# Graph attention on one core: the closing scaling and store, one destination block at a time

## The chip, the cores and the metric

The kernel runs on one core of a Trainium2 chip. Its engines work side by side, each on its own queue of instructions: TensorE (PE in the profile, with its weight loads as PEld), VectorE (DVE), ScalarE (ACT), GpSimd (POOL) and SyncE (SP), which here only issues DMAs. The metric is the device time of one execution in microseconds (us).

## The reference

A graph has 4096 nodes with 64 features and 50,000 edges. For each of 4 heads the features are projected (64 to 64), every edge gets a score from its two ends, and each destination node receives the average of its sources' projections, weighted with the exponential of the score:

```python
for h in range(n_heads):
    x_proj[h] = x @ weight[h]
    src_att = np.sum(x_proj[h, src_nodes] * att_src[h], axis=-1)
    dst_att = np.sum(x_proj[h, dst_nodes] * att_dst[h], axis=-1)
    edge_scores[h] = src_att + dst_att
edge_scores = np.where(edge_scores > 0, edge_scores, 0.2 * edge_scores)
...
        output[h, dst] += np.exp(edge_scores[h, i]) * x_proj[h, src]
...
            total = np.sum(np.exp(edge_scores[h, edges_to_dst]))
            output[h, dst] /= (total + 1e-8)
return output.transpose(1, 0, 2).reshape(num_nodes, -1)
```

So the result is a matrix of 4096 rows (destinations) by 256 columns (4 heads of 64), in 32-bit floats.

## The kernel before

The first half of the time goes into sorting the edges by destination, on VectorE. The second half, where the change lies, walks over the destinations in 33 blocks (`ND`) of 125 (`BD`); block 32, the last, has 96. Since the weighted average commutes with the projection, the kernel sums the weighted features first (`acc`) and projects the sum of each block afterwards.

`Blocks.run` is the loop over the blocks; one turn `b` of it is called step `b` here. The order is written out by hand: each engine takes its instructions in the order in which the code names them, and the steps of different blocks are interleaved.

- `load(b + 4)` has SyncE issue a DMA of 1 MB into a tile `bc` (four buffers): the sorted edges of a later block, spread over all partitions.
- `onehot(b + 2)` lets VectorE turn `bc` into matrices of zeros and ones (`oh`), in two parts: L471 for the first 4096 columns, L474 for the other 2048.
- `gather(b + 1, c)`, in three chunks `c`, lets TensorE multiply these with the node tables (L492, L494, L498) into `ps`. ScalarE takes the exponentials from it (`ex`, L500) and copies the features (`xs`, L502).
- `weights(b + 1)` picks the edge weight (`wv`, L512) and `values(b)` multiplies it with the features (`val`, L520), both on VectorE.
- `sums(b, -1)` adds up the weights on TensorE (L538); `sums(b, 0)` and `sums(b, 1)` add up the weighted features into `acc`, 32 products in all (L545). ScalarE then copies `acc` into `aT` (L602, `take`). In block 32 these go through other tiles, in parts.

What is done with a finished block is in the class `Finish`. `project(b - 1)`, placed in step `b` behind the first chunk of the gather, has TensorE multiply `aT` with the weights into the tile `pf` (L606). `invert` takes the reciprocals of the summed weights on VectorE (`inv`, L611), `give` multiplies `pf` with them into `res` on VectorE (L618) and issues the stores of the result (L622): on SyncE's queue, and for the last block one half on SyncE's and one on ScalarE's.

Before the change a tile `aT`, `pf`, `inv` or `res` holds two blocks. `project` runs in each step and fills one half of `pf`; `invert` and `give` run in the even steps from step 2 on, for blocks `b - 2` and `b - 1` together. `pf` has a single buffer (the pool `ps_f`, `bufs=1`), while `aT`, `inv` and `res` have two (the pool `fin`, `bufs=2`). When a buffer is taken anew, its writer waits for the last reader of what it held.

Inside a step, VectorE's order is: `val`, reciprocal (even steps), first part of `oh`, `wv`, second part of `oh`, scaling (even steps). Steps 1 to 3 add four small instructions at their end, which unpack the windows of later blocks (L416 to L420). TensorE's order is: first chunk of the gather, projection, sums of the weights, second and third chunk, sums of the features.

The functions that the diff touches are used once more, in a part that runs only if the edges are spread so unevenly that a window overflows; with these inputs it is not entered. The class `Total` belongs to that part.

Of the kernel before, what the change touches and what calls it, by code (L numbers as in the profile page):

```python
# [11 lines left out]
P = 128  # L12
ALPHA = 0.2
F32 = mybir.dt.float32
BF16 = mybir.dt.bfloat16
I32 = mybir.dt.int32
OP = mybir.AluOpType
# [10 lines left out]
BD = 125  # L28
# [4 lines left out]
def av(a, off, *dims):  # L33

    return dataclasses.replace(a, offset=a.offset + off, ap=[list(a.ap[0])] + [list(d) for d in dims])
# [3 lines left out]
def kernel(ctx: ExitStack, tc: tile.TileContext, x: bass.AP, edge_index: bass.AP,  # L39
                         weight: bass.AP, att_src: bass.AP, att_dst: bass.AP, out: bass.AP):  # L40
    nc = tc.nc
    V, S, G, T = nc.vector, nc.scalar, nc.gpsimd, nc.tensor
    N, Din = x.shape
    H, _, Dout = weight.shape
    E = edge_index.shape[1]
    NB = N // P
    ND = -(-N // BD)
    NI = -(-ND // 8)
    SG = N // NR
    C = H * Dout  # L50
# [122 lines left out]
    Wbd = cst.tile([P, 2, P], F32)  # L173
# [7 lines left out]
    class Sorter:  # L181


        def __init__(self, pool, first):
            self.a = [first, pool.tile([P, L], F32, name="sA"), pool.tile([P, L], F32, name="sB")]
            self.cur = 0
            self.y = pool.tile([P, L], F32, name="sY")
            self.z = pool.tile([P, L], F32, name="sZ")
# [121 lines left out]
    def whole(pool, t, up, what):  # L310

        i = pool.tile([P, NI], I32, name=f"whole{what}")
        V.tensor_scalar(out=i[:], in0=t[:], scalar1=float(up), scalar2=None, op0=OP.add)
        V.tensor_scalar(out=i[:], in0=i[:], scalar1=FINE, scalar2=FINE, op0=OP.logical_shift_right,
                        op1=OP.logical_shift_left)
        V.tensor_copy(out=t[:], in_=i[:])
# [26 lines left out]
    def group(pool, pp, start, spy=None):  # L343

        raw = pool.tile([P, L], F32, name="raw")
        fetch(pool, skey1, start, W1, raw, 1)
        kr = pool.tile([P, L], F32, name="kr")
        S.activation(out=kr[:], in_=raw[:], func=ACTF.Identity, bias=goff[:, 0:1])
        sgn = below(pool, kr[:], L, nb2, ND, 8 * NI)
        so = Sorter(pool, raw)  # L350
        so.rows(9)
        cps = counts(pool, pp, sgn, 8 * NI, [sel2[:]])
        ki = pool.tile([P, L], I32, name="ki")
        store(skey2, so.runs(ki, FINE, spy))
        bounds(pool, cps, 8 * NI, L, off2, m8, 8, ws2, we2)
        whole(pool, ws2, 0, 0)
# [46 lines left out]
    AW = 2 * BD + H  # L403
# [26 lines left out]
    class Blocks:  # L430
# [129 lines left out]
        def run(self, first=0, also={}):  # L560
            for b in range(first, ND):
                self.load(b + 4)
                self.values(b, 2 if b == ND - 1 else 1)
                self.gather(b + 1, 0)
                if b:
                    self.sink.project(b - 1)
                self.sums(b, -1)
                self.gather(b + 1, 1)
                self.gather(b + 1, 2)

                pair = b and b % 2 == 0
                if pair:
                    self.sink.invert(b - 2, 2)
                self.onehot(b + 2, halves=(0,))
                self.weights(b + 1)
                self.onehot(b + 2, halves=(1,))
                if pair:
                    self.sink.give(b - 2, 2)
                self.sums(b, 0)
                self.sums(b, 1)  # L580
                if b in also:
                    also[b]()
            self.sink.project(ND - 1)
            n = 2 - ND % 2
            self.sink.invert(ND - n, n)
            self.sink.give(ND - n, n, 2)

    class Finish:


        def __init__(self, ctx):
            self.first = eps
            self.apart = True
            self.aT, self.pf = {}, {}
            self.fp = ctx.enter_context(tc.tile_pool(name="fin", bufs=2))
            self.psf = ctx.enter_context(tc.tile_pool(name="ps_f", bufs=1, space=PSUM))

        def take(self, b, acc, at=0):
            if b % 2 == 0 and acc.shape[-1] != BD:
                self.aT[b // 2] = self.fp.tile([P, 2, AW], F32, name="aT")  # L600
                self.pf[b // 2] = self.psf.tile([P, 2, C], F32, name="pf")
            S.copy(out=self.aT[b // 2][:, b % 2, at:at + acc.shape[-1]], in_=acc)  # L602

        def project(self, b):
            for k in range(2):
                T.matmul(out=self.pf[b // 2][:, b % 2, k * P:(k + 1) * P], lhsT=self.aT[b // 2][:, b % 2, k * BD:k * BD + P],  # L606
                         rhs=Wbd[:, k, :], start=(b % 2 == 0 and k == 0), stop=True, skip_group_check=True)

        def invert(self, b, n):
            self.inv = self.fp.tile([P, 2, H], F32, name="inv")  # L610
            V.reciprocal(out=self.inv[0:BD, 0:n], in_=self.aT[b // 2][0:BD, 0:n, 2 * BD:AW])  # L611

        def give(self, b, n, parts=1):
            res = self.fp.tile([P, 2, H, Dout], F32, name="res")
            nh = H // parts
            for k, eng in zip(range(parts), (nc.sync, nc.scalar)):
                h = slice(k * nh, (k + 1) * nh)
                V.tensor_tensor(out=res[0:BD, 0:n, h], in0=av(self.pf[b // 2][0:BD], k * nh * Dout, [C, n], [Dout, nh], [1, Dout]),  # L618
                                in1=av(self.inv[0:BD], k * nh, [H, n], [1, nh], [0, Dout]), op=OP.mult)
                for i in range(n):  # L620
                    m = min(BD, N - (b + i) * BD)
                    eng.dma_start(out=out[(b + i) * BD:(b + i) * BD + m, k * nh * Dout:(k + 1) * nh * Dout],  # L622
                                  in_=res[0:m, i, h].rearrange("p h o -> p (h o)"))

    class Total:

# [9 lines left out]
        def project(self, b):  # L636
            pass

        def invert(self, b, n):
            pass  # L640

        def give(self, b, n, parts=1):
            pass

    def advance(pool, ws, we, w, what):

        n = ws.shape[1]
        at = pool.tile([P, n], F32, name=f"at{what}")
        gone = pool.tile([P, n], F32, name=f"gone{what}")
        V.tensor_tensor(out=gone[:], in0=ws[:], in1=we[:], op=OP.is_ge)  # L650
        V.tensor_scalar(out=at[:], in0=ws[:], scalar1=-1.0, scalar2=float(P * L), op0=OP.mult, op1=OP.add)
        V.tensor_tensor(out=at[:], in0=at[:], in1=gone[:], op=OP.mult)
        V.tensor_tensor(out=at[:], in0=at[:], in1=ws[:], op=OP.add)
        V.tensor_scalar(out=ws[:], in0=ws[:], scalar1=float(w), scalar2=None, op0=OP.add)
        return at
# [86 lines left out]
    with tc.If((n1 > W1) | (n2 > W2)):  # L742
        with tc.tile_pool(name="all", bufs=1) as al:
            total = al.tile([P, ND, AW], F32)
            V.memset(total[:], 0.0)
            with tc.For_i(0, n1, W1):
                at1 = advance(al, ws1, we1, W1, 1)
                with tc.tile_pool(name="sort3", bufs=1) as so3, tc.tile_pool(name="pp3", bufs=1, space=PSUM) as pp3:
                    group(so3, pp3, at1[:])
                    whole(so3, we2, (1 << FINE) - 1, 1)  # L750
                    longest(so3, pp3, (ws2, we2))
                m2 = room(1, L)
                with tc.For_i(0, m2, W2):
                    with ExitStack() as st:
                        win = Windows(st.enter_context(tc.tile_pool(name="win", bufs=1)), advance(al, ws2, we2, W2, 2)[:])
                        for i in range(NI):
                            win.unpack(i, nc.sync, nc.scalar)
                        blocks = Blocks(st, Total(total))
                        for b in range(4):
                            blocks.load(b)  # L760
                        blocks.onehot(0)
                        blocks.start()
                        blocks.run()
            with ExitStack() as st:
                V.tensor_scalar(out=total[:, :, 2 * BD:AW], in0=total[:, :, 2 * BD:AW], scalar1=1e-8, scalar2=None,
                                op0=OP.add)
                fin = Finish(st)
                for b in range(ND):
                    fin.take(b, total[:, b, :])
                    fin.project(b)  # L770
                    if b % 2 or b == ND - 1:
                        fin.invert(b - b % 2, b % 2 + 1)
                        fin.give(b - b % 2, b % 2 + 1)


# [28 lines left out]
```

## Time and profile before

| | us |
|---|---|
| median of 14 runs | 298.91 |
| lowest and highest of them | 295.94 and 300.15 |
| the profiled execution's own time | 296.66 |
| its span, from the first to the last instruction | 294.7 |

| engine | busy us | share of the span |
|---|---|---|
| PE (products) | 202.6 | 69% |
| PEld (weight loads) | 193.7 | 66% |
| VectorE | 260.6 | 88% |
| ScalarE | 186.0 | 63% |
| GpSimd | 28.1 | 10% |

The profile shows one execution. It divides the span into 40 equal slices and prints the busy share of each engine in tenths, 9 for 90% or more; PEclk is the clock granted to TensorE in the same tenths. A group of instructions is one line of the code on one engine: what it writes and reads, how often it ran, its busy time and the mean of one in ns, and behind the bar the time for which the engine was idle just before, and what ended it. In a timeline the columns are the start in us, the duration in us, engine, line and operation; an idle time before an instruction stands in brackets with what ended it. In the list of waits the three numbers are us in total, times and the longest. "issue" means that the profile shows nothing that the engine waited for. Consecutive instructions of an engine may overlap a little: the next one can start before the end of the one ahead is reported.

### The profile page before, as it was taken

What the parts mean: (1) busy time and instruction counts of PE and PEld (TensorE: products, weight loads), DVE (VectorE), ACT (ScalarE), POOL (GpSimd) and SP (SyncE); (2) the same over time, 40 slices, a digit from 0 to 9 for tenths busy, and PEclk for the clock granted to TensorE, in tenths of its full rate; (3) what the DMA queues carried; (4) which work ended last, traced back from release to release, by engine and by line L of the source; (5) the groups of instructions that cost most, each with busy time, mean ns of one, the idle gap of its engine ahead of it and who ended that gap; (6) DMA issues with size and microseconds to landing.
All of it is one profiled execution on the core that took longest, in us unless ns stands there. A gap on an engine that the chain in (4) does not pass through costs nothing.

```text
span 294.7 us, 8453 instructions
## 1 busy us (share of the span) xinstructions
PE 202.6 (69%) x3541; PEld 193.7 (66%) x3541; DVE 260.6 (88%) x504; ACT 186.0 (63%) x361; POOL 28.1 (10%) x78
## 2 busy tenths in 40 slices
PE   0001899960000007669999999999999999999980
PEld 0000599960000005569899999999999999999980
DVE  5999999995599999679999999999999999999960
ACT  2950710040599935857778787878787778777850
POOL 7882000001100002400000000000000000000000
PEclk9999985555555555899999999999999999999997
DMA  3025000000100001294767755775578556854012
GB/s 109 1 62 100 0 2 0 0 1 37 36 0 0 0 0 42 67 410 164 253 247 308 244 214 216 295 275 194 219 285 285 186 229 270 293 204 180 9 37 59
DMA packets 13326, 40.75 MB, mean 138 GB/s; under 512 B 3120, under 2 KB 8912, under 8 KB 9312
## 3 DMA queue, kind: packets, MB, share of 16 engines
q1 hardware_dynamic: 10768, 37.91, 35.2%
q10 hardware_dynamic: 1808, 1.56, 2.3%
q0 software_dynamic: 704, 0.66, 1.0%
q8 instruction: 30, 0.49, 0.7%
q14 instruction: 16, 0.13, 0.1%
HBM read 35.08 MB, written 5.05 MB: 136 GB/s over the span
## 4 chain that ended last, share of the span: by engine, by line
PE 50%; DVE 40%; issue 3%; DMA 2%; ACT 2%; DVEq 0%; POOL 0%; POOLq 0%; ACTq 0%
PE acc L545 17%; DVE sA L210 13%; DVE sB L210 12%; PE ps L494 10%; PE pf L606 6%; PE ps L492 6%; PE ps L498 5%; PE acc L538 4%; DVE val L520 2%; DVE sB L239 1%; DVE oh L471 1%; DMA eS<-in_edge_index_dram 1%; ACT xs L502 1%; DMA raw<-gat_sorted,wi 1%; DVE sA L199 1%
## 5 line engine op out<-in xcount | busy, mean ns | idle before, releaser
L502 ACT CAST xs<-ps 128x1200 bf16<-128x1200 f32 (+1 forms) x99 | 104.0, 1051 | 0.0
L520 DVE TENSOR_TENSOR val<-xs,wv 128x4096 bf16<-128x4096 bf16 (+1 forms) x34 | 75.4, 2220 | 1.0 <-ACT xs L502 1.0
L545 PE MATMUL acc<-xs,val 128*128 128x125 bf16 x1024 | 61.8, 218 | 1.9 <-issue 1.5
L494 PE MATMUL ps<-adb,oh 128*128 128x136 bf16 x528 | 62.7, 225 | 0.0
L492 PE MATMUL ps<-xa,oh 128*128 128x72 bf16 x528 | 59.9, 198 | 2.6 <-DVE oh L471 2.3
L545 PEld LDWEIGHTS <-val 128*128 128x128 bf16 x1056 | 58.8, 98 | 2.4 <-issue 1.7
L494 PEld LDWEIGHTS <-oh 128*128 128x128 bf16 x528 | 49.8, 99 | 0.5 <-issue 0.4
L492 PEld LDWEIGHTS <-oh 128*128 128x128 bf16 x528 | 47.5, 99 | 2.9 <-DVE oh L471 2.9
L500 ACT ACTIVATE ex<-ps 128x96 bf16<-128x96 f32 (+1 forms) x99 | 24.9, 252 | 33.0 <-PE ps L498 32.9
L471 DVE TENSOR_SCALAR oh<-bc,pF 128x4096 bf16<-128x4096 bf16 (+2 forms) x37 | 42.4, 1145 | 0.3 <-ACT bc L458 0.3
L210 DVE TENSOR_TENSOR sA<-sB 128x256 f32<-128x256 f32 (+2 forms) x104 | 37.2, 399 | 1.7
L210 DVE TENSOR_TENSOR sB<-sA 128x256 f32<-128x256 f32 (+2 forms) x98 | 35.1, 399 | 1.6
L498 PE MATMUL ps<-xa,oh 128*128 128x72 bf16 x528 | 33.8, 199 | 0.0
L292 PE MATMUL cnt_ps<-sgn,sel 128*128 128x17 f32 (+1 forms) x6 | 1.7, 390 | 42.0 <-ACT sgn L284 42.0
L292 PEld LDWEIGHTS cnt_ps<-sgn,sel 128*128 128x128 f32 x6 | 1.4, 318 | 42.1 <-issue 42.0
L498 PEld LDWEIGHTS <-oh 128*128 128x128 bf16 x528 | 26.7, 100 | 0.1
L474 DVE TENSOR_SCALAR oh<-bc,pF 128x2048 bf16<-128x2048 bf16 (+2 forms) x37 | 25.5, 689 | 0.0
L395 PEld LDWEIGHTS at_ps<-uv,xT 64*128 64x128 f32 x130 | 24.7, 297 | 0.4 <-issue 0.4
L395 PE MATMUL at_ps<-uv,xT 64*128 64x4 f32 x130 | 24.8, 328 | 0.0
L606 PE MATMUL pf<-Wbd,aT 128*128 128x128 f32 x132 | 22.7, 294 | 2.7 <-ACT aT L602 0.8
L281 ACT ACTIVATE junk<-kr,nb 128x512 f32<-128x512 f32 x33 | 23.8, 722 | 1.1
L606 PEld LDWEIGHTS pf<-Wbd,aT 128*128 128x128 f32 x132 | 17.3, 191 | 4.5 <-issue 3.4
(139 smaller groups left out, 214.1 us busy)
## 6 DMA issues: line engine op xcount, KB each, us to landing
bc<-gat_bins SPq DMA_DIRECT2D x31, 1024.0 KB, 9.1
out_dram<-res SPq DMA_DIRECT2D x32, 125.0 KB
eD<-in_edge_index_dram ACTq DMA_DIRECT2D x2, 195.0 KB
eS<-in_edge_index_dram SPq DMA_DIRECT2D x2, 195.0 KB
gat_bins<-tb SPq DMA_DIRECT2D x10, 32.0 KB
gat_sorted<-sA SPq DMA_DIRECT2D x1, 256.0 KB
gat_sorted<-ki SPq DMA_DIRECT2D x1, 256.0 KB
win<-gat_sorted,wi POOLq DMA_INDIRECT x5, 2.6
```

The costliest lines, as they stand in the source:

```text
L210: V.tensor_tensor(out=av(d[:], o, [2 * h, n], [1, h]), in0=av(s[:], 0, [2 * h, n], [1, h]), in1=av(s[:], h, [2 * h, n], [1, h]), op=op)
L395: T.matmul(out=ps[:, b, :], lhsT=xT[:, b * step:b * step + P], rhs=uv[:, k, :], start=(b == 0), stop=True, skip_group_check=True)
L471: V.tensor_scalar(out=oh[:, 0:2, e], in0=bc[:, :, e], scalar1=pF[:, 0:1], scalar2=None, op0=OP.is_equal)
L474: V.tensor_scalar(out=oh[:, 2, e], in0=bc[:, 1, e], scalar1=pF[:, 1:2], scalar2=None, op0=OP.is_equal)
L492: T.matmul(out=ps[:, i, P:P + XC], lhsT=oh[:, 1, e], rhs=xa[:, 2 * t, :], start=(i % 2 == 0), stop=False, skip_group_check=True)
L494: T.matmul(out=ps[:, i, 0:S0], lhsT=oh[:, 0, e], rhs=adb[:, b, :], start=False, stop=False, skip_group_check=True)
L498: T.matmul(out=ps[:, i, P:P + XC], lhsT=oh[:, 2, t * W2:(t + 1) * W2], rhs=xa[:, 2 * t + 1, :], start=False, stop=True, skip_group_check=True)
L500: S.activation(out=av(ex[:], 2 * t0, [2, n], [2 * NT, 2 * H], [1, 2]), in_=av(ps[:], P, [PW, n], [1, 2 * H], [0, 2]), func=ACTF.Exp)
L502: S.copy(out=xs[:, t0:t0 + n, 0:P + XC], in_=ps[:, 0:n, 0:P + XC])
L520: V.tensor_tensor(out=av(val[:], h * Dout, [Dout, n], [C, NT], [1, Din]), in0=av(xs[:], S0, [0, n], [XW, NT], [1, Din]), in1=av(wv[:], h * ...
L545: T.matmul(out=self.to[k], lhsT=val[:, t, k * P:(k + 1) * P], rhs=xs[:, t, 0:BD], start=apart and t == 0, stop=(t == NT - 1), skip_group_c ...
L606: T.matmul(out=self.pf[b // 2][:, b % 2, k * P:(k + 1) * P], lhsT=self.aT[b // 2][:, b % 2, k * BD:k * BD + P], rhs=Wbd[:, k, :], start=(b ...
```

## The change

Each tile of `Finish` now holds one block. `take` opens an `aT` for every block, `project` opens a `pf` for every block, and `invert` and `give` run in every step from step 1 on, for block `b - 1`, whose projection is in the same step ahead of them. Scaling and reciprocal cover 256 and 4 columns instead of 512 and 8, and there is one store after each. The numbers of buffers in the pools stay as they were: one for `pf`, two for `aT`, `inv` and `res`. The last block was alone before and is handled as before.

```diff
@@ class Blocks, run
-                pair = b and b % 2 == 0
-                if pair:
-                    self.sink.invert(b - 2, 2)
+                if b:
+                    self.sink.invert(b - 1)
                 self.onehot(b + 2, halves=(0,))
                 self.weights(b + 1)
                 self.onehot(b + 2, halves=(1,))
-                if pair:
-                    self.sink.give(b - 2, 2)
+                if b:
+                    self.sink.give(b - 1)
                 self.sums(b, 0)
                 self.sums(b, 1)
...
             self.sink.project(ND - 1)
-            n = 2 - ND % 2
-            self.sink.invert(ND - n, n)
-            self.sink.give(ND - n, n, 2)
+            self.sink.invert(ND - 1)
+            self.sink.give(ND - 1, 2)
@@ class Finish
         def take(self, b, acc, at=0):
-            if b % 2 == 0 and acc.shape[-1] != BD:
-                self.aT[b // 2] = self.fp.tile([P, 2, AW], F32, name="aT")
-                self.pf[b // 2] = self.psf.tile([P, 2, C], F32, name="pf")
-            S.copy(out=self.aT[b // 2][:, b % 2, at:at + acc.shape[-1]], in_=acc)
+            if acc.shape[-1] != BD:
+                self.aT[b] = self.fp.tile([P, AW], F32, name="aT")
+            S.copy(out=self.aT[b][:, at:at + acc.shape[-1]], in_=acc)
 
         def project(self, b):
+            self.pf = self.psf.tile([P, C], F32, name="pf")
             for k in range(2):
-                T.matmul(out=self.pf[b // 2][:, b % 2, k * P:(k + 1) * P], lhsT=self.aT[b // 2][:, b % 2, k * BD:k * BD + P],
-                         rhs=Wbd[:, k, :], start=(b % 2 == 0 and k == 0), stop=True, skip_group_check=True)
-
-        def invert(self, b, n):
-            self.inv = self.fp.tile([P, 2, H], F32, name="inv")
-            V.reciprocal(out=self.inv[0:BD, 0:n], in_=self.aT[b // 2][0:BD, 0:n, 2 * BD:AW])
-
-        def give(self, b, n, parts=1):
-            res = self.fp.tile([P, 2, H, Dout], F32, name="res")
+                T.matmul(out=self.pf[:, k * P:(k + 1) * P], lhsT=self.aT[b][:, k * BD:k * BD + P], rhs=Wbd[:, k, :],
+                         start=(k == 0), stop=True, skip_group_check=True)
+
+        def invert(self, b):
+            self.inv = self.fp.tile([P, H], F32, name="inv")
+            V.reciprocal(out=self.inv[0:BD], in_=self.aT.pop(b)[0:BD, 2 * BD:AW])
+
+        def give(self, b, parts=1):
+            res = self.fp.tile([P, H, Dout], F32, name="res")
+            m = min(BD, N - b * BD)
             nh = H // parts
             for k, eng in zip(range(parts), (nc.sync, nc.scalar)):
                 h = slice(k * nh, (k + 1) * nh)
-                V.tensor_tensor(out=res[0:BD, 0:n, h], in0=av(self.pf[b // 2][0:BD], k * nh * Dout, [C, n], [Dout, nh], [1, Dout]),
-                                in1=av(self.inv[0:BD], k * nh, [H, n], [1, nh], [0, Dout]), op=OP.mult)
-                for i in range(n):
-                    m = min(BD, N - (b + i) * BD)
-                    eng.dma_start(out=out[(b + i) * BD:(b + i) * BD + m, k * nh * Dout:(k + 1) * nh * Dout],
-                                  in_=res[0:m, i, h].rearrange("p h o -> p (h o)"))
+                V.tensor_tensor(out=res[0:BD, h], in0=av(self.pf[0:BD], k * nh * Dout, [Dout, nh], [1, Dout]),
+                                in1=av(self.inv[0:BD], k * nh, [1, nh], [0, Dout]), op=OP.mult)
+                eng.dma_start(out=out[b * BD:b * BD + m, k * nh * Dout:(k + 1) * nh * Dout],
+                              in_=res[0:m, h].rearrange("p h o -> p (h o)"))
```

The scaling, L618 before, is L617 in the changed kernel; its store, L622, is L619; the projection, L606, is L604; the reciprocal, L611, is L609; and the copy, L602, is L599.

## The prediction

> **What bounds the kernel now.** I read the page's engine shares and slices first, to find the stage that holds the change, and then the timeline of one pair of steps inside it.
>
> ```profile
> PE 202.6 (69%) x3541; PEld 193.7 (66%) x3541; DVE 260.6 (88%) x504; ACT 186.0 (63%) x361; POOL 28.1 (10%) x78
> PE   0001899960000007669999999999999999999980
> DVE  5999999995599999679999999999999999999960
> PEclk9999985555555555899999999999999999999997
> ```
>
> VectorE has the larger share over the span, but that is the sort in the first half. The change lies in the second half (slices 19 to 39), where TensorE is full too, at full granted clock. The chain of waits gives the rhythm there: each line is the start of one step's 32 weighted sums.
>
> ```profile
> 150.46 1.84 PE acc L545 x32
> 155.49 1.76 PE acc L545 x32
> 160.20 1.76 PE acc L545 x32
> 165.21 1.76 PE acc L545 x32
> 169.92 1.76 PE acc L545 x32
> ...
> 281.85 1.77 PE acc L545 x32
> ```
>
> Steps of 4.71 and 5.01 us alternate: from step 5 (155.49) to step 31 (281.85) are 26 steps in 126.36 us, 4.86 each. So one step in two loses 0.30 us. The list of waits and the timeline of steps 16 and 17 say to what:
>
> ```profile
> PEld pf L606 <- issue: 3.4, 15, 0.2
> ```
> ```profile
> 206.18 0.29 PEld L498 LDWEIGHTS <-oh 128*128 128x128 bf16 x6
> 206.40 0.53 PEld L606 LDWEIGHTS pf<-Wbd,aT 128*128 128x128 f32 x4
> 209.81 0.22 DVE L512 TENSOR_TENSOR wv<-ex 128x128 bf16<-128x128 bf16 x1 [0.36 <-ACT ex L500]
> 209.95 0.74 DVE L474 TENSOR_SCALAR oh<-bc,pF 128x2048 bf16<-128x2048 bf16 x1
> 210.61 0.68 DVE L618 TENSOR_TENSOR res<-pf,inv 125x512 f32<-125x512 f32 x1
> 210.89 0.29 PEld L498 LDWEIGHTS <-oh 128*128 128x128 bf16 x6
> 211.21 2.28 DVE L520 TENSOR_TENSOR val<-xs,wv 128x4096 bf16<-128x4096 bf16 x1
> 211.41 0.52 PEld L606 LDWEIGHTS pf<-Wbd,aT 128*128 128x128 f32 x4 [0.23 <-issue]
> ```
>
> In the even step the projection (L606) follows 0.22 us behind the start of the six loads of L498. In the odd step it would start at 210.89 + 0.22 = 211.11, but starts at 211.41. Just before, at 210.61 + 0.68 = 211.29, the scaling of the pair (L618) ended. The page calls the idle time "issue", but the cause can be read from the code: `pf` has one buffer, an odd step's projection opens a new pair, and so it must wait until L618 has read the old pair. From the end of L618 to the projection are 0.12 us.
>
> **The change, part by part.** I measure in one step's frame: c is the time at which the last L498 of the second gather ends (208.31 in step 16). From there `wv` starts at c + 1.50, the scaling at c + 2.30, and an unhindered projection of the next step at c + 2.80. From a projection to the next c are 208.31 - 206.40 = 1.91.
>
> *Scaling in halves.* Durations of both shapes are in the groups by form:
>
> ```profile
> L618 DVE TENSOR_TENSOR res<-pf,inv 125x512 f32<-125x512 f32 x16 | 10.9, 682 | 0.1
> L618 DVE TENSOR_TENSOR res<-pf,inv 125x128 f32<-125x128 f32 x2 | 0.5, 285 | 1.2 <-PE pf L606 1.2
> L611 DVE RECIPROCAL inv<-aT 125x8 f32<-125x8 f32 x16 | 3.1, 194 | 0.0
> L611 DVE RECIPROCAL inv<-aT 125x4 f32<-125x4 f32 x1 | 0.2, 168 | 0.0
> ```
>
> (682 - 285)/384 = 1.034 ns an element, so 256 elements take 285 + 128 x 1.034 = 417 ns. The bounds are the two rows themselves, 0.29 and 0.68; I take 0.42, since it lies between two rows of the same operation.
>
> *The wait of the projection.* It is no longer in every second step: with one block to a `pf`, every projection opens a new tile and waits for the scaling of the step before. It can start at c + 2.30 + 0.42 + 0.12 = c + 2.84 against c + 2.80 unhindered: 0.04 late in each step, in place of 0.30 late in each second. A step is then 2.84 + 1.91 = 4.75 us. A second thing sits at the same place. The projection waits for two engines, which costs it a semaphore instruction of its own on TensorE's queue (18 of 51 ns each in the trace, so far in odd steps). Where the wait is late it lies inside the 0.12; were it on time, it would add up to 0.05, so 4.71 is hardly reachable. I take 4.755.
>
> *VectorE.* It gains work, and it had little room. By starts of successive instructions (they begin about 0.08 before the one ahead ends), a step after the change is: `wv` 0.14, second half of `oh` 0.66, scaling 0.42 - 0.08 = 0.34, `val` 2.20, reciprocal 0.11, first half of `oh` 1.15: 4.60 us. The same sum for the pair before is 4.27 in the odd step (without scaling) and 4.80 in the even one (0.60 for the scaling), 4.535 on average, so splitting costs some 0.07 a step. It fits under 4.755 with 0.15 to spare, which `wv` will show as waiting for ScalarE. Here a rule speaks against the change: the Trainium skill (VectorE: DVE Perf Modes, The TRN2 errata) gives each VectorE instruction a fixed term of some 150 cycles, exposed between instructions, and advises large tiles. Two more instructions per pair would be 2 x 0.156 = 0.31 us, 0.156 a step, and the step 4.535 + 0.156 = 4.69. The durations agree with the fixed term (285 - 128 x 1.034 = 153 ns), but the starts overlap it in part, so I use 4.60. By either, VectorE stays below TensorE's rhythm; without that cover each hundredth costs 0.26 us over the 26 steps.
>
> *What is late next.* `val` is the instruction behind the scaling. It starts at c + 2.64 and ends at c + 4.92; the sums that need it would start at c + 4.75 + 0.30 = c + 5.05. The handover took 0.06 to 0.15 in steps 3 and 4, so it fits to within 0.02 us.
>
> *ScalarE.* `aT` now turns over every two blocks, so each copy (L602) gets a wait for VectorE's reciprocal. That reciprocal lies a whole step earlier, so the wait itself is over; the extra semaphore instruction (17 ns each at L500) falls where ScalarE waits for the sums anyway. Bounds: 0 and 0.02 a step; I take 0, as the copy ends 0.14 before the projection starts.
>
> *DMAs and SP's queue.* Their number and sizes stay: 33 blocks, 125 KB each. They are moved: one store, one load, instead of two stores and then two loads issued together (211.32 and 212.04). A load (1 MB, landing 9.1 us after issue as half of a pair) sits behind the store of the step before; it goes out after the scaling and is first read by the `oh` three steps on: 213.41 - 211.29 = 2.1 us to that of the next step, and two steps more, 11.6 us. That covers 9.1, and a single one should land earlier. A `res` buffer used to return after four steps, now after two: a store has 2 x 4.75 - 0.42 = 9.1 us to land. The landing of SP's stores is not shown; the one on ScalarE's queue took 3.4. The skill (DMA: Bandwidth & Descriptors, Queues, rings and completion order) says that descriptors are consumed in ring order on each DMA engine, so a store can sit behind an unfinished load: bounds 3.4 and 3.4 plus what is left of a 9.1 us load after a 4.75 us step, 7.8. Both fit. Price: nothing.
>
> *The start of the stage.* Steps 1 to 4 are bound by VectorE, because the unpacking of the windows (four instructions, 0.60 us by starts) lies in the first three. There the change costs. Steps 1 and 3 gain a scaling and a reciprocal (0.45 each, of which step 1 hides the reciprocal's 0.11 in a wait); steps 2 and 4 trade 0.60 for 0.34. At `val` of step 4 VectorE stands 0.34 - 0.26 + 0.11 + 0.34 = 0.53 late. TensorE's sums of step 4 start at about 150.95 and those of step 5, with no stall of the projection, at 150.95 + 4.71 = 155.66, 0.17 later than before.
>
> *The end.* The last block was scaled by itself already. In step 31 the scaling falls into the 0.49 us in which `val` waits for ScalarE (0.34 fits), so the end moves with the sums of step 31.
>
> *Sum.* Sums of step 31 at 155.66 + 26 x 4.755 = 279.29 instead of 281.85: 2.56, rounded to 2.6 us. The profiled execution goes from 296.66 (span 294.7, 2 us around it) to 294.1, a ratio of 0.991. The runs' median is 298.91, 0.8% above the profiled one; I take off the same amount: 296.3. The runs spread over 4.2 us by themselves, which a range has to carry. No change can be told from one within 0.5% (1.5 us).
>
> **Rivals.**
>
> (A) The wait is hidden altogether: 4.71 a step, 155.66 + 26 x 4.71 = 278.12, gain 3.7, 295.2. For it: only 0.04 us is missing. Against: the semaphore instruction in every step.
>
> (B) The gain is eaten: `val` or the scaling a few hundredths later than worked out. At 4.82 the sums of step 31 come at 280.98, gain 0.9: 298.0. For it: three chains (projection, `val`, VectorE's queue) end within 0.15 us of each other. Against: each comes from rows in this trace.
>
> (C) Slower: the projection's wait stays as long as it was, now in every step. The place is L606; the price is 0.30 x 26 with the pair's 0.30 x 13 taken off. If the scaling of half the elements, with its waits, held `pf` as long as the whole one (0.68), each step would take 5.01: 155.66 + 26 x 5.01 = 285.9, 4.1 slower, 303.0. It decides from a step of (281.85 - 155.66)/26 = 4.853, a scaling of 0.52 us. For it: twice as many such waits, and the fixed 153 ns. Against: 128 elements took 0.285, so 0.52 lies 0.10 above the line. Smaller excesses give 299 to 301.
>
> (D) Stores land too late for the two `res` buffers: the scaling would wait and TensorE after it. It takes a landing above 9.1 us; at 10 us each pair of steps loses 0.9, 13 times: 12 slower, less the gain, 308. For it: the landing is unseen. Against: the idle stretch of the DMA engines ahead of each pair of stores.
>
> **How the numbers follow.** Main case 0.55 (own range 295.3 to 297.5), A 0.12, B 0.17, C 0.11, D 0.05. A and the main case are faster by over 0.5%, save a tenth or so of the latter: 0.63 (0.12 + 0.51). Same: B and that rest, 0.20. Slower: C and D with a little of B, 0.17. The range goes from 294.6 (A with the runs' spread) to 299.7 (B, and the mild half of C); left out are D, most of C and the far low end.
>
> **What would show it.** Right: sums 4.75 apart in every step, no more alternation; L617 at 0.42 us, 33 blocks; the idle time ahead of the projection in every step and under 0.1; `wv` waiting some 0.1 to 0.15 for ScalarE; the stage entered 0.2 later. Wrong: steps of 4.86 or more, a scaling over 0.5, `val` as the releaser of the sums in most steps, or scalings that wait for a store.

## The result and the profile after

The changed kernel takes 293.65 us (median of 10 runs, 293.06 to 295.51) against 297.16 us for the kernel before (median of 47 runs by now, 295.94 to 300.15). The ratio is 0.9875, with a 95% interval from 0.9839 to 0.9910: faster by 1.25%, clear of the 0.5% that a measurement can tell. The direction was right and the gain larger than forecast: 3.5 us instead of 2.6. The time itself lies 1.0 us below the low end of the range, 294.6.

The page of the changed kernel, with a span of 293.0 us (the execution took 295.25), engine shares and slices:

```profile
PE 204.6 (70%) x3541; PEld 196.9 (67%) x3541; DVE 262.7 (90%) x536; ACT 185.9 (63%) x361; POOL 29.4 (10%) x78
PE   0001899970000006779999999999999999999991
DVE  5999999995599999677999999999999999999970
PEclk9999965555555557595999999999999999999998
```

VectorE has 2.1 us and 32 instructions more. In slices 17 and 19 TensorE's clock stands at 0.5 again, which it did not in the profile before; more of that below. The starts of the weighted sums in the chain of waits, one line a step, columns start, length and work:

```profile
157.32 1.76 PE acc L545 x32
162.06 1.76 PE acc L545 x32
166.80 1.76 PE acc L545 x32
171.54 1.76 PE acc L545 x32
...
271.08 1.76 PE acc L545 x32
```

The alternation of 4.71 and 5.01 us is gone: every step is 4.74 (4.755 was forecast). The timeline of one step around the projection, now L604, and the scaling, now L617:

```profile
216.01 0.41 DVE L617 TENSOR_TENSOR res<-pf,inv 125x256 f32<-125x256 f32 x1
216.29 0.29 PEld L498 LDWEIGHTS <-oh 128*128 128x128 bf16 x6
216.34 2.28 DVE L520 TENSOR_TENSOR val<-xs,wv 128x4096 bf16<-128x4096 bf16 x1
216.54 0.52 PEld L604 LDWEIGHTS pf<-Wbd,aT 128*128 128x128 f32 x4
```

The projection starts 0.25 behind L498, where 0.22 is the unhindered distance: it is 0.03 late in each step, in place of 0.30 in each second one. The idle time of 3.4 us that the list of waits showed at the projection is gone from it. The groups by form:

```profile
L617 DVE TENSOR_TENSOR res<-pf,inv 125x256 f32<-125x256 f32 x32 | 13.3, 417 | 0.1
L609 DVE RECIPROCAL inv<-aT 125x4 f32<-125x4 f32 x33 | 5.6, 170 | 0.0
```

The scaling takes 417 ns, as interpolated from the two rows before.

### The profile page after: what moved, and what is told of

It is laid out like the page before. It is cut to its first block, busy times and chain, and to the rows that moved or that the text cites. A ratio compares the mean times of both kernels' runs of the same rounds, so it can differ in the third digit from the quotient of the medians.

```text
span 293.0 us, 8545 instructions
## 1 busy us (share of the span) xinstructions
PE 204.6 (70%) x3541; PEld 196.9 (67%) x3541; DVE 262.7 (90%) x536; ACT 185.9 (63%) x361; POOL 29.4 (10%) x78
## 4 chain that ended last, share of the span: by engine, by line
PE 48%; DVE 41%; issue 3%; ACT 3%; DMA 2%; DVEq 0%; POOL 0%; POOLq 0%; ACTq 0%
PE acc L545 17%; DVE sA L210 13%; DVE sB L210 12%; PE ps L494 9%; PE pf L604 6%; PE ps L492 5%; PE ps L498 5%; PE acc L538 4%; DVE oh L471 2%; DVE val L520 2%; DVE sB L239 1%; ACT xs L502 1%; DMA eS<-in_edge_index_dram 1%; DVE oh L474 1%; DMA raw<-gat_sorted,wi 1%
## 5 line engine op out<-in xcount | busy, mean ns | idle before, releaser
L498 PE MATMUL ps<-xa,oh 128*128 128x72 bf16 x528 | 34.2, 200 | 0.0
L498 PEld LDWEIGHTS <-oh 128*128 128x128 bf16 x528 | 27.2, 101 | 0.0
L395 PEld LDWEIGHTS at_ps<-uv,xT 64*128 64x128 f32 x130 | 26.3, 313 | 0.2 <-issue 0.2
L395 PE MATMUL at_ps<-uv,xT 64*128 64x4 f32 x130 | 26.4, 340 | 0.0
L604 PE MATMUL pf<-Wbd,aT 128*128 128x128 f32 x132 | 23.1, 299 | 0.8 <-ACT aT L599 0.8
L378 PE MATMUL ps<-ident,wS 64*128 64x64 f32 x2 | 0.7, 350 | 28.0 <-DMA wS<-in_weight_dram 28.0
```

Of the source, the lines that this page charges most:

```text
L395: T.matmul(out=ps[:, b, :], lhsT=xT[:, b * step:b * step + P], rhs=uv[:, k, :], start=(b == 0), stop=True, skip_group_check=True)
L498: T.matmul(out=ps[:, i, P:P + XC], lhsT=oh[:, 2, t * W2:(t + 1) * W2], rhs=xa[:, 2 * t + 1, :], start=False, stop=True, skip_group_check=True)
L604: T.matmul(out=self.pf[:, k * P:(k + 1) * P], lhsT=self.aT[b][:, k * BD:k * BD + P], rhs=Wbd[:, k, :], start=(k == 0), stop=True, skip_gro ...
```

## The experiments

The runs below were made on several chips, and the chips differ: the kernel before took 296.98 us on one and 301.9 on another (medians). Each ratio is to the kernel before on the same chip, with its 95% interval in brackets; where no ratio is given, one profiled execution shows the length of the steps.

**The spread of the runs.** The kernel before, with no edit.

> The kernel before, unchanged, to see where its runs' spread of 4.2 us comes from. Theory 1 (TensorE's clock at the entry of the second half): the runs fall into groups some 3 us apart, the longer ones with the lower mean granted clock, about 0.01 per 1.5 us, as in the runs of the changed kernel (290.6 us span at 0.865, 293.2 at 0.842). Theory 2 (something outside TensorE, such as DMA latency): long and short runs show the same mean clock. The pairs of steps are 9.72 us in every one that is profiled.

The runs fit theory 1. Of the 14, eleven have spans of 294.1 to 294.9 us with a mean granted clock of 0.855 to 0.867; the other three have 295.5 at 0.856, 296.6 at 0.843 and 298.3 at 0.842. (Another 44 runs of it on this chip fill the space between, so these are not separate groups.) Windows at the entry of the second half show the clock of two profiles there: length, busy TensorE, then granted clock, DMA share and GB/s. First the kernel before as shown in the prediction, then the changed kernel as shown above:

```profile
118.00:124.00 6.00, 3.60 (x40) 0.85 0.25 60
124.00:130.00 6.00, 4.52 (x87) 1.00 0.85 352
130.00:138.00 8.00, 6.92 (x138) 1.00 0.72 272
```
```profile
118.00:124.00 6.00, 4.24 (x27) 0.50 0.24 66
124.00:130.00 6.00, 4.40 (x86) 0.99 1.00 317
130.00:138.00 8.00, 7.44 (x99) 0.57 0.75 291
```

In the second execution the clock falls to half once more, from about 131 to 138 us. The sums of step 5 start at 157.32 instead of 155.49, 1.83 us later. Most of that is there already at the sums of step 1, ahead of which VectorE has none of the added instructions; first the kernel before, then the changed one:

```profile
135.19 1.93 PE L545 MATMUL acc<-xs,val 128*128 128x125 bf16 x32
```
```profile
136.83 2.37 PE L545 MATMUL acc<-xs,val 128*128 128x125 bf16 x32
```

At the sums of step 0, ahead of the half clock, the second execution was still 0.38 us early (130.08 against 130.46). So 1.64 of the 1.83 us come ahead of the change and go with the clock; the other 0.19 are taken up below. For this reason the two profiles differ by only 1.7 us, although the change gains about twice as much. The pairs of steps in the new profile of the kernel before are 9.72 us again.

**How long `pf` is held.** Three edits change when the projection may start, and one adds the same work without holding `pf`. The first was meant to free the halves of `pf` one by one, in the kernel before:

```diff
+            if b == 0:
+                self.pf = self.psf.tile([P, 2, C], F32, name="pf")
...
-                V.tensor_tensor(out=res[0:BD, 0:n, h], in0=av(self.pf[b // 2][0:BD], ...512 columns...
+                for i in range(n):
+                    V.tensor_tensor(out=res[0:BD, i, h], in0=av(self.pf[0:BD], ((b + i) % 2) * C + ...256 columns...
```

> The kernel before with its pairs (reciprocal of 8 columns, two stores together in every second step), but the two halves of pf come free one by one: the pair is scaled by two instructions of 256 columns, back to back, and a projection waits for the one that reads its own half. Theory 1 (the release of pf is what the change gains): the odd step's projection waits for the first of the two, 0.42 instead of 0.68 us, so the pair of steps takes 4.71 + 4.74 = 9.45 instead of 9.72, 13 x 0.27 = 3.5 us less, ratio 0.988. Theory 2 (VectorE's work spread evenly over the steps, or the DMAs spread evenly): both stay bunched here, VectorE even gains 0.08 us per pair, so 9.72 and ratio 1.000.

Neither happened: 5.07 and 4.71 in turn, ratio 1.0054 [1.0029, 1.0080], slower. The halves are not freed apart. The wait that the framework sets for the projection counts up to the second of the two scalings, so `pf` is held for both:

```profile
220.59 0.75 DVE L620 TENSOR_TENSOR res<-pf,inv 125x256 f32<-125x256 f32 x2
221.45 0.30 PEld L607 LDWEIGHTS pf<-Wbd,aT 128*128 128x128 f32 x2 [0.29 <-issue]
```

The premise of the edit was wrong, but the run is a dose of its own: 0.75 us of scaling instead of 0.68, and the odd step grew from 5.01 to 5.07. The same holds for two slots in the changed kernel (`pf[:, b % 2]` of one tile):

> The changed kernel with two slots for pf in turn (the two halves of one tile), so that a projection waits for a scaling of two steps ago, long done; its semaphore instruction stays. Theory 1 (the 0.03 us by which the step of 4.74 exceeds 4.71 are the rest of the wait): 4.71 in every step, 26 x 0.03 = 0.8 us less than the changed kernel, ratio to the kernel before 0.985. Theory 2 (they are the semaphore instruction on TensorE's queue): 4.74, ratio 0.9875 as for the changed kernel.

It measured 4.74 and 0.9910 [0.9872, 0.9947], but decides nothing: its projection still starts 0.25 us behind L498, so it still waits for the scaling just ahead. Next, the scaling done twice, both times out of `pf`, and, for comparison, a second instruction of the same shape that reads the weights instead:

```diff
+                tmp = self.fp.tile([P, H, Dout], F32, name="tmp")
+                V.tensor_tensor(out=tmp[0:BD, h], in0=av(self.pf[0:BD], ...), in1=av(self.inv[0:BD], ...), op=OP.mult)
                 V.tensor_tensor(out=res[0:BD, h], in0=av(self.pf[0:BD], ...
```
```diff
                 V.tensor_tensor(out=res[0:BD, h], in0=av(self.pf[0:BD], ...
+                tmp = self.fp.tile([P, H, Dout], F32, name="tmp")
+                V.tensor_tensor(out=tmp[0:BD, h], in0=av(Wbd[0:BD], ...), in1=av(self.inv[0:BD], ...), op=OP.mult)
```

> The changed kernel with the scaling done twice, both times reading pf (the first result goes into a tile that nobody reads): pf is held 0.34 us longer, and VectorE has 0.34 us more per step. Theory 1 (the wait for pf sets the step): scaling ends at c + 2.30 + 0.34 + 0.42 = c + 3.06, projection at c + 3.17, step 3.17 + 1.91 = 5.08 us; with the idle time ahead of the projection in every step, about 0.3 us. Theory 2 (VectorE's work sets the step): 4.60 + 0.34 = 4.94.

> The changed kernel with one more VectorE instruction of the same shape per step behind the scaling, which reads the weights in SBUF instead of pf: VectorE has the same 0.34 us more, but pf comes free as before. Theory 1 (the order counts, not the sum): no wait at the projection; VectorE's own 4.94 us are now the bound, so 4.94 per step and not 5.08, with the sums waiting for val. Theory 2 (a wait for pf in any case): 5.08 as with the doubled scaling. If VectorE had the slack that its idle time suggests (0.1), 4.84.

Measured: 5.07 us per step when `pf` is held, 4.93 when it is not. The lists of waits of the two, in this order, over the steady steps:

```profile
PEld pf L604 <- issue: 6.8, 23, 0.3
PE pf L604 <- DVE res L620: 4.5, 23, 0.2
```
```profile
PEld L545 <- DVE val L520: 4.2, 25, 0.2
```

The first waits at the projection, 0.3 us each time; the second never does, and its sums wait for `val`, because VectorE itself has become the bound. So the step is the longest of three things: TensorE's own work without a wait (4.71), VectorE's work (4.60 + 0.33 = 4.93 here), and the chain from `wv` over the scaling to the projection and round to the next `wv`. This was rival C in small doses: the price of `pf` held longer is paid in full, in every step.

**Place instead of halving.** If only the release of `pf` counts, moving the scaling up must do as well as halving it. Two places were tried: right behind the reciprocal (first the changed kernel, then the kernel before with its pairs), and between the first part of `oh` and `wv`.

```diff
                 if b:
                     self.sink.invert(b - 1)
+                    self.sink.give(b - 1)
                 self.onehot(b + 2, halves=(0,))
                 self.weights(b + 1)
                 self.onehot(b + 2, halves=(1,))
-                if b:
-                    self.sink.give(b - 1)
```

> The changed kernel with the scaling moved up on VectorE, right behind the reciprocal and ahead of the first part of oh; pf comes free 2.5 us earlier. Theory 1 (rest of the wait): 4.71 per step, ratio 0.985, provided that VectorE's 4.60 us per step really fit. Theory 2 (semaphore instruction): 4.74, ratio 0.9875. Theory 3 (VectorE has no slack at this place: wv comes late by what the scaling takes, and the gather's and the sums' products after it): 4.75 to 4.9, ratio 0.988 to 1.000.

> The kernel before with its pairs and its one 512-column scaling, moved up on VectorE right behind the reciprocal: pf is free long before the odd step's projection. Theory 1 (the release of pf is what counts, not the halving): the 0.30 us stall is gone; VectorE's even step holds 4.80 us and passes on some 0.1 us, so 9.42 to 9.52 per pair instead of 9.72, ratio 0.987 to 0.992. Theory 2 (the even spread over the steps counts): 9.7, ratio 1.000.

The first gave 4.79 per step and 0.9966 [0.9940, 0.9992], theory 3: worse than the change. In its timeline the scaling waits for the reciprocal ahead of it, on the same engine:

```profile
214.81 0.17 DVE L608 RECIPROCAL inv<-aT 125x4 f32<-125x4 f32 x1
215.06 0.42 DVE L616 TENSOR_TENSOR res<-pf,inv 125x256 f32<-125x256 f32 x1
215.40 1.28 DVE L471 TENSOR_SCALAR oh<-bc,pF 128x4096 bf16<-128x4096 bf16 x1
```

From reciprocal to scaling are 0.25 us, where 0.09 to 0.11 had passed to an instruction that didn't need its result. With that, and 0.05 more for `oh` behind the scaling, VectorE's step is 4.79. The pairs there take 4.71 + 4.90 = 9.61, and the ratio is 0.9999 [0.9975, 1.0022]. The steps save 13 x 0.11 = 1.4 us by the trace, and the times don't show it. Part of it is lost at the start of the stage: from the sums of step 1 (140.45) to those of step 5 (161.35) this version takes 20.90 us, the kernel before 20.30 in both its profiles. Where the rest goes stays open, since the kernel before was not profiled on that chip.

The place between `oh` and `wv` has the reciprocal well behind it:

```diff
                 self.onehot(b + 2, halves=(0,))
+                if b:
+                    self.sink.give(b - 1)
                 self.weights(b + 1)
                 self.onehot(b + 2, halves=(1,))
-                if b:
-                    self.sink.give(b - 1)
```

and likewise with `if pair:` and `give(b - 2, 2)` in the kernel before. Beside both, on the same chip, ran the changed kernel as it is.

> The changed kernel with the scaling put between the first part of oh and wv on VectorE. There the reciprocal is long done (moving the scaling right behind it had exposed 0.14 us of waiting for it), wv has 0.11 us to spare, and pf comes free at c - 2.9 of the step that needs it at c + 2.8. So the projection's wait is over in every case, while its semaphore instruction stays. Theory 1 (the 0.03 us above 4.71 are the rest of the wait for pf): 4.71 per step, 0.8 us less than the changed kernel, ratio to before 0.985. Theory 2 (they are the semaphore instruction): 4.74, the same time as the changed kernel, 0.9875. If VectorE's 4.60 do not fit here either: over 4.75.

> The kernel before with its pairs, the one 512-column scaling moved to between the first part of oh and wv. pf is free long before the odd step's projection, and work and stores stay bunched in every second step. Theory 1 (only the release of pf counts): wv is some 0.15 us late in even steps, which the second part of oh and val can take; 9.42 to 9.50 us per pair instead of 9.72, ratio 0.987 to 0.991, as good as the change. Theory 2 (the even spread of VectorE's work or of the DMAs is what the change gains): 9.6 to 9.7, ratio 0.996 or more.

> The changed kernel again, beside the two others on the same chip. Steps of 4.74 us, ratio to before 0.9875. Its runs fall into groups by TensorE's granted clock at the entry of the second half, as the runs of the kernel before did (294.1 to 294.9 us span at 0.855 to 0.867, 296.6 to 298.3 at 0.842): some 290.5 to 291.5 at 0.855 to 0.867, 293 at 0.845. In a run with the higher clock the sums of step 5 start at about 155.5, 0.2 later than in the kernel before at the same clock; at the lower clock 1.5 to 2 later.

| | step, us | ratio to before | interval |
|---|---|---|---|
| changed kernel | 4.74 | 0.9903 | 0.9881 to 0.9925 |
| pairs, scaling moved | 4.71, every step | 0.9887 | 0.9864 to 0.9910 |
| changed kernel, scaling moved | 4.71 | 0.9834 | 0.9809 to 0.9860 |

The pairs with the scaling moved, in the chain of waits and in the timeline:

```profile
264.33 1.76 PE acc L545 x32
269.05 1.76 PE acc L545 x32
273.76 1.76 PE acc L545 x32
```
```profile
213.05 0.68 DVE L618 TENSOR_TENSOR res<-pf,inv 125x512 f32<-125x512 f32 x1
214.58 0.28 PEld L498 LDWEIGHTS <-oh 128*128 128x128 bf16 x6
214.80 0.53 PEld L606 LDWEIGHTS pf<-Wbd,aT 128*128 128x128 f32 x4
```

The whole scaling of 0.68 us is still there, VectorE's work and the stores are still bunched in every second step, and yet the steps are 4.71 us without alternation. So the even spread of work is not what the change gains; the release of `pf` is. The third line of the table beats both kernels: 297.07 us against 298.76 for the changed kernel and 301.9 for the kernel before on this chip. Its 26 steps account for 0.6 of the 1.7 us to the changed kernel; two of its six runs also had a clock of 0.856. The changed kernel had 0.837 to 0.852 here, so the groups expected of it didn't show.

One thing in these expectations was wrong: in the versions with the scaling moved, the projection's semaphore instruction is gone with the wait (3 and 4 are left in the two whole traces). A likely reason, by the order in the code, is that TensorE has by then waited for a later instruction of VectorE; it was not tested. These versions therefore don't tell the rest of the wait from that instruction.

**The last 0.03 us.** The changed kernel with half of the columns left out:

```diff
-            nh = H // parts
+            nh = H // 2 if parts == 1 else H // parts
```

> The changed kernel with only the first 128 of 256 columns scaled and stored (the other half of the result, except in the last block, is left out): the scaling ends 0.13 us sooner, at c + 2.59, and with 0.12 for the handover the projection may start at c + 2.70, before it would in any case (c + 2.80). The semaphore instruction of the projection stays in every step, as its order shows. Theory 1 (the 0.03 us above 4.71 are the rest of the wait for the scaling): 4.71 per step. Theory 2 (they are the semaphore instruction, 51 ns on TensorE's queue): 4.74.

It takes 4.71 us per step, with the semaphore instruction present in every step (51 ns each). The projection is back at 0.22 behind L498:

```profile
213.63 0.28 DVE L617 TENSOR_TENSOR res<-pf,inv 125x128 f32<-125x128 f32 x1
213.91 0.29 PEld L498 LDWEIGHTS <-oh 128*128 128x128 bf16 x6
214.13 0.53 PEld L604 LDWEIGHTS pf<-Wbd,aT 128*128 128x128 f32 x4
```

The 0.03 us were the rest of the wait, and the instruction costs nothing there.

**The landing of the stores.** The changed kernel with one buffer for `res` (a pool of its own, `bufs=1`).

> The changed kernel with a single buffer for res, so that a scaling waits until the store of the step before has landed; this measures the landing of SP's stores, which no profile showed. 4.74 - 0.33 = 4.4 us pass from a store's issue to the next scaling. Landing under 4.4: steps stay at 4.74. Landing 3.4 as on ScalarE's queue: no change. Landing up to 7.8 (behind an unfinished load): steps of up to 8 us, TensorE idle ahead of each projection. With two buffers the bound is 9.1, so either result says how near that case was.

The steps stay at 4.74, so a store lands within the 4.3 us from its issue to the next scaling. Only at the end does the scaling wait, since the last block's comes close behind that of block 31 (2.0 us in the changed kernel); the timeline of that place:

```profile
289.00 3.38 SPq L620 DMA_DIRECT2D out_dram<-res  x2
291.74 0.49 DVE L618 TENSOR_TENSOR res<-pf,inv 125x128 f32<-125x128 f32 x2 [2.68 <-DMA out_dram<-res]
```

The store issued at 289.00 freed the buffer for 291.74: 2.7 us, with no load in flight. Rival D, which needed over 9.1, was far off.

**The end of the kernel.** From the start of the sums of step 31 to the end of the span, the kernels in pairs take 12.76 to 12.97 us (five profiles), those block by block 12.16 to 12.48 (nine, the one with a single `res` buffer aside). The last block's scaling starts 6.3 us behind those sums in both kernels, so the difference lies behind it, where the stores are waited for. Three runs on the version with the scaling moved looked for the cause. The first issues the store of block 30 from within `give` of block 31:

> The version with the scaling between oh and wv, whose only change is that the store of block 30 is issued right ahead of that of block 31, as in the kernel before (res has three buffers for it). Theory 1 (the end is shorter block by block because only one store of 125 KB, not two, is queued ahead of the last ones): SyncE's last wait 3.4 us as in the kernel before instead of 2.6, and 12.7 to 13.0 us from the start of the sums of step 31 to the end, instead of 12.2. Theory 2 (the difference has another cause, such as where the scaling of the end stands): 2.6 to 2.9 and 12.2 to 12.5.

It came to 12.23 and a last wait of 2.6, but says nothing: SyncE had nothing else queued ahead and issued that store as soon as its data were there. The other two hold it back by data, or delay the single one:

```diff
+                if b == ND - 3:
+                    self.kept = res
+                    continue
+                if b == ND - 2:
+                    tmp = self.fp.tile([P, H, Dout], F32, name="tmp")
+                    V.tensor_copy(out=tmp[0:BD], in_=self.kept[0:BD])
+                    eng.dma_start(out=out[(b - 1) * BD:b * BD, :], in_=tmp[0:BD]...)
```
```diff
+                if b == ND - 2:
+                    tmp = self.fp.tile([P, H, Dout], F32, name="tmp")
+                    V.tensor_tensor(out=tmp[0:BD, h], in0=av(self.pf[0:BD], ...), ...)
                 V.tensor_tensor(out=res[0:BD, h], in0=av(self.pf[0:BD], ...
```

> The version with the scaling between oh and wv, in which the store of block 30 leaves from a copy that VectorE makes behind the scaling of block 31, so that both stores are issued together some 5.0 us behind the start of the sums of step 31, as in the kernel before. (The run that was to do this left the store where it was: SyncE's queue issued it as soon as block 30 was scaled, since nothing stood ahead of it.) Theory 1 (two stores in a row ahead of the last one, begun late): SyncE's last wait 3.4 us instead of 2.6, 12.7 to 13.0 us from the start of the sums of step 31 to the end, instead of 12.2. Theory 2 (another cause): 2.6 to 2.9 and 12.2 to 12.5.

> The same version with block 31 scaled twice, so that its one store is issued about 0.33 us later, 5.0 us behind the start of the sums of step 31; the store of block 30 leaves early. Theory 1a (the number of stores in a row counts): last wait 2.6 to 2.7, 12.2 to 12.3 us. Theory 1b (only the late begin counts): 3.0 to 3.4, 12.5 to 13.0 us.

Two stores in a row: 12.74 us; one late store: 12.21. SyncE's last wait, for the stores still out, in the two:

```profile
SPq L746 <- SPq L746: 3.2, 1, 3.2
```
```profile
SPq L743 <- SPq L743: 2.7, 1, 2.7
```

It is 3.4 in the kernel before and 2.9 in the changed one. Two full stores ahead of the last halves, instead of one, cost about 0.5 us, by one execution of each version. The ends of versions with one store differ by up to 0.3 among themselves (12.44 and 12.26 in two profiles of the changed kernel); why stays open.

## Why the prediction was right in kind and wrong in its numbers

**What bounds the kernel** stood: TensorE, with VectorE close behind, and one stall in two steps at the projection. The cause read from the code, that `pf` waits for L618, is shown by the doses: 0.29, 0.42 and 0.75 us of scaling gave steps of 4.71, 4.74 and 5.07, and the whole 0.68 us, moved ahead of `wv`, gave 4.71.

**Scaling in halves**: 0.417 was worked out and measured.

**The wait of the projection**: forecast 0.04 late in each step, measured 0.03. The step was 0.015 us too long, 26 x 0.015 = 0.4 us: 0.01 by the size of the wait, and 0.005 by the addition for the semaphore instruction. That addition, which made 4.71 "hardly reachable", was wrong: with the wait met in time, the instruction cost nothing.

**VectorE**: its 4.60 us held; with 0.33 added the trace showed 4.93. The rule of the Trainium skill (VectorE: DVE Perf Modes, The TRN2 errata) led to an estimate of 0.156 us a step for two more instructions per pair; by the starts in the trace it is 0.07. The page counts some 150 cycles in the duration of an instruction and speaks of latency exposed between instructions for those that read SBUF; the prediction put the two together for every instruction. With this price the step of the run with 0.33 more would have been 4.69 + 0.33 = 5.02; 4.93 decides for the starts. So does the pair scaled in two halves: 0.75 us instead of 0.68, 0.07 for one instruction more. What lay behind VectorE, `val`, was never the releaser in the steady steps.

**ScalarE, the DMAs, SP's queue**: nothing, as forecast. A load landed after 6.5 us (median) instead of 9.1, a store in 2.7 at the end and under 4.3 in the steps.

**The start of the stage**: forecast 0.17 us later at the sums of step 5. Counted from the sums of step 1, these sums come 20.30 us later in both profiles of the kernel before (135.19 to 155.49 in the first), and 20.49 and 20.52 in the two of the changed kernel (136.83 to 157.32; 140.37 to 160.89, at full clock all the way): 0.2 later, as forecast.

**The end**: "the end moves with the sums of step 31" failed. The end comes 0.4 us sooner (12.85 to 12.44 from those sums), by the runs on the end because one full store, not two, is queued ahead of the last halves. The stores were followed through the steps but not to the last of them.

**Sum.** With 4.74 a step and the end: 26 x (4.86 - 4.74) = 3.1, less 0.2, plus 0.4: 3.3 us inside the span. On the chip where the versions ran side by side the median span fell by 3.5 (299.9 to 296.4), but the median time only by 3.1 (301.9 to 298.76). The rest lies outside the span: the kernel before takes 1.9 us there (42 of 44 runs on one chip within 1.85 to 1.95), the changed one 2.4 (its first twelve runs, 2.25 to 2.52), where the prediction left "2 us around it" as they were. The profile does not show this time, and its cause is open; the version with the scaling right behind the reciprocal has 1.9 again. So 2.6 was short by 0.4 for the step and 0.4 for the end, and as much as one of these was lost outside the span. That the medians of the result differ by 3.5 all the same may in part be luck: it depends on how many runs of lower clock each holds, and the clocks of those 47 runs are not all known. Side by side the ratio is 0.9903, close to the 0.991 of the sum.

**From the profiled time to the median** is the step that put the time out of the range. The sum made 296.66 into 294.1. The prediction then scaled this to the median of 14 runs, 298.91, and took 296.3. But 8 of those 14 runs lay between 298.9 and 300.2, where the runs with the lower clock lie (298.5 and 300.2 in the run of this kernel above; the clocks of the 14 were not listed). Of the next 33 runs only 8 lay there, and with all 47 the median is 297.16. Of the 2.65 us between 296.3 and the measured 293.65, this level is 1.75 and the gain 0.9. Against 294.1 the measured time would have been 0.4 off. The range carried a spread on top of 298.91, instead of letting the level itself fall back to the profiled execution's.

**Rivals.** A (4.71 a step) came near the gain with 3.7, but by luck: the step stayed at 4.74. B didn't happen. C is real as a mechanism, and 0.75 us of scaling in pairs already made the kernel slower. D was excluded by the landing times.

## What to carry to other kernels

A stall in every second step of a loop, on an engine that is otherwise full, is worth following to the last reader of a single buffer: what counts is when that reader ends, so moving it ahead of work that nobody waits for can do as much as making it shorter, and here both together did best. A change in how stores are issued should be followed to the end of the queue too, where the last transfers are waited for. And before a sum is scaled to a median, ask whether the runs are of one kind: where their clocks differ, the runs with the clock of the profiled execution are the ones to compare with.

## What was not expected of the hardware

- TensorE's granted clock at the entry of the second half differs between executions of one program. In one profile of the changed kernel its last stretch at half was from about 131 to 138 us (the sums of step 5 at 157.32), in the other from 123 to 133 (those sums at 160.89). In the first, 1.64 us went with it; on one chip the longer of 14 runs of the kernel before show the lower mean clock.
- A VectorE instruction that needs the result of the one just ahead started 0.25 us behind that one's start, instead of 0.09 to 0.11 for one that doesn't (behind a reciprocal of 0.17 us).
- Two halves of one `pf` tile, read by two instructions, are not released apart in this framework: the writer waits for the later reader.
- A store of 125 KB from 125 partitions released its buffer 2.7 us after its issue, with no load in flight.
- Outside the profiled span, the kernel before took 1.9 us and the changed one 2.4; the cause is open.
